# Padded tables that bring regions and weight rings to multiples of 256 bytes, and a small block of the recurrence's inverse kept in a chain buffer

## The chip, the cores and the metric

One core of one Trainium2 chip. The metric is device time in microseconds (us) of one execution; lower is better. The runs of the kernel before lie at 2445.13, 2445.94 and 2451.08 us, the median is 2445.94 us.

## What is computed

Two blocks on a sequence of 256 tokens with 2048 channels, float32 in and out. The first block has two layers: an RWKV-7 mixer (four projections, two small LoRA paths, a recurrence over time in 32 heads of 64, a projection back) and a differential attention (shared K and V, 8 heads, a gate, a projection back), each followed by a layer norm of a weighted residual. The second block puts 16 learned tokens ahead (272 rows), projects to pool, convolution and gate channels, mixes them, and ends in an MLP with a squared ReLU:

```python
y = _rwkv7_mixer(x, ...)                       # layer 0: r, k, v, g projections, recurrence, w_out
x = _layernorm(ALPHA * x + y, ...)
k_sh, v_sh = x @ w_k_shared, x @ w_v_shared
y = _diff_mixer(x, k_sh, v_sh, ...)            # layer 1
x = _layernorm(ALPHA * x + y, ...)
h = concat([meta, x]); u = rms_norm(h)
proj = u @ w_in                                # pool, conv value, conv gate, gate a, gate b
m = sigmoid(ga) * y_pool + sigmoid(gb) * y_conv
h = h + rms_norm(m @ w_o)
f = square(relu(rms_norm(h) @ w_up)) @ w_down
return (h + rms_norm(f))[META:]
```

The recurrence is computed in chunks of 64 steps. Each chunk needs the inverse of a triangular 64 x 64 matrix, put together from two 32 x 32 inverses and a product of three 32 x 32 blocks.

## The kernel before

Activations are kept transposed: channels on the 128 partitions, 16 tiles of them side by side, tokens along the row. They live in long-lived *regions* of 128 partitions (B0, B1, B2, B3, H0, L0, taken by `region`, line 196), which are used again by stage after stage under new names. The profile shows B regions as rB, H0 as rH, L0 as rL.

**Projections.** Every float32 product is made of three matmuls in a faster float format: weights and activations are split into a high part and a low rest, and `mm3` (line 313) issues high x high, high x low rest of the activation, low rest of the weight x high. The weights stream in tiles of 128 x 1024 (512 KB): the SP queue loads them into `wraw`, ScalarE copies the high part into `wh` (line 283), VectorE, in some stages every second time GpSimd, subtracts it into `wl` (line 284). Each of the three is a ring of three buffers of 4096 bytes a partition. `proj` (line 323) walks over 16 column tiles (or more) and 16 k; the weights are loaded into TensorE (128 x 128), and 256 token columns, in the second block's input projection 272, stream past them. The order of the weights is one list (line 228), from which `WS` runs ahead by its rings' depth. In V and in the MLP's down projection activations are the stationary side and 512 columns of a weight tile stream (line 127, `mm`). A matmul with one stationary and one moving tile is written acc<-moving,stationary in the profile.

In the last projection five of the last eight weight tiles are split into buffers of their own (`own0h` to `own2l` and, for the first two, parts of region L0), so that they need not wait for the ring.

**The recurrence.** `wkv(j)` (line 705) is a generator, one for each of 16 pairs of heads, run a little at every tick between the projections' matmuls. It loads what `pregen` and `invgen` stored, forms the product of two 32 x 32 blocks on TensorE, copies it to `Q` (lines 740 to 742), multiplies it by the third block and puts the result into `Z` (lines 755 to 764), and then runs a chain of four chunks (lines 807 to 842) whose left-hand matrices are in `BG`, one of three buffers of [4 chunks, 2 heads, 2, 64]. Before the change Q has a tile of its own, `wQ`, 512 bytes a partition in one buffer. `take` and `give` limit how many pairs are in a part at a time: one in the front part, which Q belongs to, and three in the chain, one for each BG buffer. BG[:, 3, 1] is the last chunk's matrix for the second head. For the last chunk the half of the chain's result that carries the state on is not read.

**Where the tiles lie.** Long-lived tiles stand one behind the other in the order of their making: `cst` (constants), `prm` and `prm1` (parameter vectors), the regions, EXH and EXL (two more slots for mixed activations), `der`, `omu`, `PC`, B2, B3, two buffers each of `mx` and `xx`, `sst` (a row of 272 sums), two small `rr`, and then the rings wraw, wh and wl. Behind them each stage opens a pool of its own. Small tiles are rounded up to 32 bytes. Start of a tile within a partition, in bytes past a multiple of 256:

| tile | before | after, as the sizes add up |
|---|---|---|
| cst | 128 | 128 |
| prm / prm1 | 224 / 32 | 0 / 0 |
| B0, B1, H0, L0, EXH, EXL | 160 | 0 |
| B2, B3, mx, xx, sst | 96 | 0 |
| wraw, wh, wl (all nine) | 224 | 0 |
| first tile of each stage's pool, among them ml | 224 | 0 |
| own0h to own2l (last stage) | 0 | 32 |
| zh, zl (pool groups) | 192 | 224 |

A row of 256 columns has 1024 bytes, so all 16 rows of a region start alike. A row of 272 has 1088, so rows of the second block's input start at 160, 224, 32, 96 and again, after the change at 0, 64, 128, 192. [...] In the projection after the attention (wbo) the high parts are in B1 and the low ones in B3; in the second block's output projection (wo) in B1 and ml; in K, Q, the gate and up in H0 and L0.

Of the kernel before, what the change touches and what calls it, by code (L numbers as in the profile page):

```python
# [10 lines left out]
F32 = mybir.dt.float32  # L11
# [8 lines left out]
SEQ = 256  # L20
NT = 16
META = 16
L2 = SEQ + META
# [9 lines left out]
P2048 = ["mu_k", "mu_v", "mu_r", "mu_g", "mu_w", "mu_a", "w0", "a0", "k_k", "k_a", "r_k", "gn_g", "gn_b",  # L33
         "ln_g0", "ln_b0", "ln_g1", "ln_b1", "g_pre", "g_post", "g_pre_mlp", "g_post_mlp"]
P1024 = ["pool_scale", "b_dw", "cln_g", "cln_b"]
CONSTS = [("ident", 128), ("istack", 64), ("bones", 128), ("sel2", 2), ("maskn", 128), ("maskg", 128),
          ("mask2", 128), ("scanm", 256), ("ones", 128), ("epow", 16)]
DIST_BIG = 1.0e30
INVQ = 500
LAG = 3  # L40
# [21 lines left out]
def shape_consts():  # L62
    p = np.arange(128)
    c = np.arange(128)
    o = {}
    o["ident"] = np.eye(128)
    o["istack"] = (p[:, None] % 64 == np.arange(64)[None, :])
    o["bones"] = (p[:, None] // 64 == c[None, :] // 64)
    o["sel2"] = (p[:, None] // 64 == np.arange(2)[None, :])
    o["maskn"] = -1.0 * (p[:, None] % 64 < c[None, :] % 64)  # L70
    o["maskg"] = (p[:, None] % 64 <= c[None, :] % 64)
    m2 = np.ones((128, 128))
    m2[:, 64:] = c[None, :64] < (p[:, None] % 64)
    o["mask2"] = m2
    o["scanm"] = np.broadcast_to((np.arange(256) % CH != 0)[None, :], (128, 256))
    o["ones"] = np.ones((128, 128))
    o["epow"] = np.full((128, 16), -0.5)
    out = np.concatenate([np.asarray(o[n], np.float32) for n, w in CONSTS], axis=1)
    q = np.arange(256)
    k = np.arange(256)  # L80
    dist = np.abs(q[:, None] - k[None, :]).astype(np.float32)
    dist = np.where(k[None, :] // CH <= q[:, None] // CH, dist, np.float32(DIST_BIG)).astype(np.float32)
    dd = np.concatenate([dist[:128, :128], dist[128:, :]], axis=1)
    return np.ascontiguousarray(out), np.ascontiguousarray(dd)
# [25 lines left out]
def body(ctx: ExitStack, tc: tile.TileContext, t: dict, out: bass.AP, dbg=None):  # L110
    nc = tc.nc
    S = ctx.enter_context(tc.tile_pool(name="S", bufs=1))
# [13 lines left out]
    def mm(o, l, r, start=True, stop=True):  # L126
        i = nc.tensor.matmul(o, l, r, start=start, stop=stop, skip_group_check=True)  # L127
        if hop["lag"]:
            hop["due"].append((hop["n"] + hop["lag"], i))

    def turn(o, i):

        nc.tensor.transpose(o, i, ident[:i.shape[0], :i.shape[0]])

    def tt(o, a, b, op, eng=None):
        return (eng or nc.vector).tensor_tensor(o, a, b, op)  # L136
# [58 lines left out]
    def region(tag, dt, shape):  # L195
        n = 1
        for v in shape[1:]:
            n *= v
        bw = BW.get(tag, NT * L2)
        assert n <= bw  # L200
        tl = S.tile([128, bw], dt, tag=tag, name=f"r{tag}")
        v = tl[:, :n]
        if len(shape) == 3:
            v = v.rearrange("p (a b) -> p a b", b=shape[2])
        elif len(shape) == 4:
            v = v.rearrange("p (a b c) -> p a b c", b=shape[2], c=shape[3])
        return v

    cst = S.tile([128, sum(w for _, w in CONSTS)], F32, tag="cst", name="cst")
    prm = S.tile([128, len(P2048), NT], F32, tag="prm", name="prm")  # L210
    prm1 = S.tile([128, len(P1024), 8], F32, tag="prm1", name="prm1")
    C = {}
    off = 0
    for n, w in CONSTS:
# [85 lines left out]
    def give(what):  # L300
        busy[what] -= 1
# [4 lines left out]
    def bank():  # L306
        yield from take("m")
        return mbank()
# [67 lines left out]
        s = n % NS  # L376
        return (H0[:, s], L0[:, s]) if s < NT else (EXH[:, s - NT], EXL[:, s - NT])

    derived = S.tile([128, 1, NT], F32, tag="der", name="der")
    omu = S.tile([128, 6, NT], F32, tag="omu", name="omu")  # L380
    PC = S.tile([64, NT, 2, 4], F32, tag="PC", name="PC")

# [21 lines left out]
    def f1(tag, cols, bufs=1, parts=128, dt=F32, name=None):  # L404
        return F1.tile([parts, cols], dt, tag=tag, name=name or tag, bufs=bufs)
# [297 lines left out]
    def wkv(j):  # L703
# [25 lines left out]
        BG, RZ, SS = BGB[j % NB], RZB[j % NB], SSB[j % NB]  # L729
# [7 lines left out]
        for c in range(4):  # L737
            mm(kp[:, c * 128:c * 128 + 128], KT[:, c], KB[:, c, 0:3:2])
        yield
        Q = f1("wQ", 128)  # L740
        nc.vector.tensor_copy(Q[32:64], qp[32:64, :128])
        nc.scalar.copy(Q[96:128], qp[96:128, :128])
        give("m")
# [11 lines left out]
        for c in range(4):  # L755
            for h in range(2):
                hs = slice(64 * h + 32, 64 * h + 64)
                mm(zp[64 * h:64 * h + 32, c * 32:c * 32 + 32], Q[hs, c * 32:c * 32 + 32], Z[hs, c, h, 32:64])
        vp = yield from bank()
# [103 lines left out]
    def wkvman():  # L863
        while wq["next"] < NT:
            j = wq["next"]
            if state["inv"] > j // 8 and wq["t"] - wq["last"] >= INTERVAL and busy.get("ld", 0) < 2:
                bg.start(wkv(j))
                wq["next"] += 1
                wq["last"] = wq["t"]
            wq["t"] += 1  # L870
            yield
# [347 lines left out]
    ul = region("L0", F32R, [128, NT, L2])  # L1219
    nc.scalar.copy(uh[:, :, 0:META], um)  # L1220
    tt(ul[:, :, 0:META], um, uh[:, :, 0:META].bitcast(F32), SUB, nc.gpsimd)
    sst = S.tile([128, L2], F32, tag="sst", name="sst")
    sq3 = {}

    def square_in(j, src, n, s2, F, eng):
# [217 lines left out]
    ss = sst[:, :SEQ]  # L1443
# [21 lines left out]
    rb = mbank()  # L1465
    for b in range(2):
        turn(rb[:, b * 128:b * 128 + 128], r[:, b:b + 1].to_broadcast([128, 128]))
    ss = S.tile([128, L2], F32, tag="sst", name="sst")[:, :SEQ]
    H = region("B3", F32, [128, NT, SEQ])
    uh = region("H0", F32R, [128, NT, SEQ])  # L1470
    ul = region("L0", F32R, [128, NT, SEQ])
# [146 lines left out]
def layout(i):  # L1618
    f = {n: np.asarray(a) for n, a in i.items()}
    o = {}  # L1620
    o["x"] = f["x"][0].T.reshape(NT, 128, SEQ).transpose(1, 0, 2)
    o["meta"] = f["meta_2"].T.reshape(NT, 128, META).transpose(1, 0, 2)
    o["consts"], o["dist"] = shape_consts()
    vec = {"mu_r": f["a_mu_proj"][0, 0], "mu_k": f["a_mu_proj"][0, 1], "mu_v": f["a_mu_proj"][0, 2], "mu_g": f["a_mu_proj"][0, 3],
           "mu_w": f["a_mu_lora"][0, 0], "mu_a": f["a_mu_lora"][0, 1], "w0": f["a_w0"][0], "a0": f["a_a0"][0],
# [31 lines left out]
def build(arrays, debug=None):  # L1657
    import concourse.bacc as _bacc

    nc = _bacc.Bacc("TRN2", target_bir_lowering=False, num_devices=1)  # L1660
    t = {}
    for name, a in arrays.items():
        t[name] = nc.dram_tensor(f"in_{name}", a.shape, mybir.dt.from_np(a.dtype), kind="ExternalInput").ap()
    out = nc.dram_tensor("out_0", (2, 128, D), F32, kind="ExternalOutput").ap()
    dbg = None
    if debug:
        dbg = {n: nc.dram_tensor(f"dbg_{n}", s, F32, kind="ExternalOutput").ap() for n, s in debug.items()}
    with tile.TileContext(nc, schedule_with_timeline_sim=True) as tc:
        body(tc, t, out, dbg)
    return nc  # L1670
# [10 lines left out]
```

## Time and profile before

| | |
|---|---|
| runs | 2445.13, 2445.94, 2451.08 us; median 2445.94 |
| profiled execution | 2448.95 us, of it 2447.1 us from the first to the last instruction |
| granted TensorE clock, mean of the span | 0.992 |
| busy: TensorE, VectorE, ScalarE, GpSimd | 2373.7, 1572.0, 1214.6, 560.9 us |
| DMA | 437.84 MB, 179 GB/s on the mean |

The profile is one execution. Engines: PE is TensorE's matmuls, PEld its weight loads, which overlap them, DVE VectorE, ACT ScalarE, POOL GpSimd, SP the queue that issues the transfers. Matmuls overlap in the pipeline: the record of one is longer than the distance to the next, so their pace is read from counts over a stretch, not from a duration.

### The profile page before, as it was taken

The page shows a single profiled execution, that of the slowest core. Times are in us where ns is not written, and L with a number is a line of the kernel's source. Part 1 is how long each engine was busy: PE and PEld are TensorE (multiplying, and loading weights), DVE is VectorE, ACT ScalarE, POOL GpSimd, SP SyncE. Part 2 cuts the span into 40 slices and gives each one's busy share as a digit, 9 for nine tenths or more (in the row PEclk, how much of TensorE's full clock was granted, in tenths as well). Part 3 has the DMA queues.
Part 4 walks back from the last instruction along what each step waited for, and adds up shares of the span by engine and source line. Part 5 has one row for each costly group of instructions (what it writes and reads, how often), then busy time and mean ns, then how long its engine had stood idle before and what let it go on. Part 6 is the DMA issues. An engine that isn't in the chain of part 4 may idle for free.

```text
span 2447.1 us, 46389 instructions
## 1 busy us (share of the span) xinstructions
PE 2373.7 (97%) x18359; PEld 2254.1 (92%) x18359; DVE 1572.0 (64%) x2675; ACT 1214.6 (50%) x2033; POOL 560.9 (23%) x583
## 2 busy tenths in 40 slices
PE   7999999999999999999999999999999999999998
PEld 6989899899978999999999999999998998998986
DVE  7788867676674455666689853454854655655655
ACT  7874556655444445554633455344544443443443
POOL 0110022331630000017766553531400000000000
PEclk9999999999999999999999999999999999999999
DMA  6577654445556654555455655555566666566655
GB/s 218 165 232 224 200 174 137 135 134 172 175 173 191 195 176 156 164 175 163 149 172 174 189 173 181 182 181 172 173 192 191 186 189 192 187 189 191 188 182 163
DMA packets 157978, 437.84 MB, mean 179 GB/s; under 512 B 45280, under 2 KB 50784, under 8 KB 157536
## 3 DMA queue, kind: packets, MB, share of 16 engines
q1 hardware_dynamic: 157760, 434.87, 57.7%
q8 instruction: 144, 2.36, 0.4%
q14 instruction: 74, 0.61, 0.1%
HBM read 418.55 MB, written 16.25 MB: 178 GB/s over the span
## 4 chain that ended last, share of the span: by engine, by line
PE 83%; DVE 5%; POOL 3%; DMA 3%; issue 2%; ACT 2%; SPq 1%; DVEq 0%; POOLq 0%; ACTq 0%
PE acc L315 58%; PE acc L127 18%; PE psm L127 5%; PE psc L127 2%; DVE wl L284 2%; POOL rB L136 1%; DMA wraw<-in_wk 1%; ACT wh L283 1%; POOL s L136 1%; DMA wraw<-in_wr 1%; POOL sst L136 1%; DVE rB L139 0%; POOL mt L136 0%; DVE rB L136 0%; DMA nd<-nb 0%
## 5 line engine op out<-in xcount | busy, mean ns | idle before, releaser
L284 DVE TENSOR_TENSOR wl<-wraw,wh 128x1024 fp32r<-128x1024 f32 x680 | 852.6, 1255 | 627.0 <-ACT wh L283 622.0
L283 ACT CAST wh<-wraw 128x1024 fp32r<-128x1024 f32 x749 | 784.2, 1048 | 880.7 <-PE acc L315 509.3
L315 PE MATMUL acc<-rH,wh 128*128 128x256 f32 (+1 forms) x4096 | 1132.9, 284 | 21.4 <-ACT wh L283 11.8
L315 PE MATMUL acc<-rL,wh 128*128 128x256 f32 (+1 forms) x3840 | 1077.3, 283 | 9.9 <-DVE rL L136 5.9
L315 PE MATMUL acc<-rH,wl 128*128 128x256 f32 (+1 forms) x3840 | 1078.3, 284 | 6.4 <-POOL wl L284 4.7
L315 PEld LDWEIGHTS acc<-rH,wh 128*128 128x128 f32 x4096 | 765.6, 190 | 27.4 <-ACT wh L283 12.7
L315 PEld LDWEIGHTS acc<-rL,wh 128*128 128x128 f32 x3840 | 726.0, 189 | 14.8 <-DVE rL L136 8.0
L315 PEld LDWEIGHTS acc<-rH,wl 128*128 128x128 f32 x3840 | 728.3, 190 | 9.9 <-POOL wl L284 5.7
L127 PE MATMUL acc<-wh,rB 128*128 128x512 f32 x984 | 306.0, 391 | 0.0
L315 PE MATMUL acc<-rB,wh 128*128 128x256 f32 x1024 | 233.5, 281 | 1.4 <-DVE mt L139 1.4
L136 POOL TENSOR_TENSOR r<-r,cst 128x4 f32<-128x4 f32 (+1 forms) x34 | 37.5, 1104 | 844.0 <-DVE r L145 688.1
L127 PEld LDWEIGHTS acc<-wh,rB 128*128 128x128 f32 x984 | 184.8, 188 | 40.8
L315 PE MATMUL acc<-rB,wl 128*128 128x256 f32 x768 | 214.0, 281 | 7.5 <-DVE wl L284 7.5
L284 POOL TENSOR_TENSOR wl<-wraw,wh 128x1024 fp32r<-128x1024 f32 x69 | 170.6, 2472 | 143.2 <-ACT wh L283 134.5
L127 PE MATMUL acc<-wl,rB 128*128 128x512 f32 x492 | 194.6, 396 | 0.0
L315 PEld LDWEIGHTS acc<-rB,wh 128*128 128x128 f32 x1024 | 174.1, 188 | 2.2 <-DVE mt L139 1.7
L315 PEld LDWEIGHTS acc<-rB,wl 128*128 128x128 f32 x768 | 144.1, 188 | 9.4 <-DVE wl L284 9.3
L127 PEld LDWEIGHTS acc<-wl,rB 128*128 128x128 f32 x492 | 92.5, 188 | 19.0
L139 DVE SCALAR_TENSOR_TENSOR psm<-aconv,wdw,psm 128x256 f32<-128x256 f32 x240 | 102.3, 483 | 0.8
L136 POOL TENSOR_TENSOR asq<-asq 128x256 f32<-128x256 f32 x8 | 5.9, 736 | 330.9 <-ACT asq L148 330.9
L315 PE MATMUL acc<-ml,wh 128*128 128x256 f32 x256 | 72.1, 282 | 0.0
L136 POOL TENSOR_TENSOR sst<-sst,sqt 128x256 f32<-128x256 f32 (+1 forms) x44 | 44.0, 1000 | 87.5 <-ACT sqt L148 86.3
(335 smaller groups left out, 2549.5 us busy)
## 6 DMA issues: line engine op xcount, KB each, us to landing
wraw<-in_wup SPq DMA_DIRECT2D x128, 512.0 KB, 4.3
wraw<-in_wdn SPq DMA_DIRECT2D x128, 512.0 KB, 3.6
wraw<-in_win SPq DMA_DIRECT2D x112, 512.0 KB, 3.6
wraw<-in_wqg SPq DMA_DIRECT2D x64, 512.0 KB, 3.6
wraw<-in_wk SPq DMA_DIRECT2D x32, 512.0 KB, 4.3
wraw<-in_wv SPq DMA_DIRECT2D x32, 512.0 KB, 4.7
wraw<-in_wr SPq DMA_DIRECT2D x32, 512.0 KB, 3.7
wraw<-in_wg SPq DMA_DIRECT2D x32, 512.0 KB, 3.6
```

Source lines behind the costliest of these rows:

```text
L127: i = nc.tensor.matmul(o, l, r, start=start, stop=stop, skip_group_check=True)
L136: return (eng or nc.vector).tensor_tensor(o, a, b, op)
L139: return nc.vector.scalar_tensor_tensor(o, a, s, b, op0, op1)
L283: c = nc.scalar.copy(h, r)
L284: s = e.tensor_tensor(l, r, h.bitcast(F32), SUB)
L315: i = nc.tensor.matmul(ps, w, x, start=f, stop=e, skip_group_check=True)
```

## The change

Three of the long-lived tables get longer, so that what lies behind them moves: 14 columns of zeros at the end of the constants, three more rows in `prm`, four in `prm1`, a second row in `derived`, and `sst` is taken as 304 columns of which 272 are used. The views that the code works on are the same. The two copies that made `wQ` write into BG[:, 3, 1] of the pair's own chain buffer, and the tile wQ is gone. The chain's mask (the product with maskg) and the copy of the transposed blocks write that buffer later.

```diff
--- before.py
+++ after.py
@@ -34,7 +34,7 @@
          "ln_g0", "ln_b0", "ln_g1", "ln_b1", "g_pre", "g_post", "g_pre_mlp", "g_post_mlp"]
 P1024 = ["pool_scale", "b_dw", "cln_g", "cln_b"]
 CONSTS = [("ident", 128), ("istack", 64), ("bones", 128), ("sel2", 2), ("maskn", 128), ("maskg", 128),
-          ("mask2", 128), ("scanm", 256), ("ones", 128), ("epow", 16)]
+          ("mask2", 128), ("scanm", 256), ("ones", 128), ("epow", 16), ("fill", 14)]
 DIST_BIG = 1.0e30
 INVQ = 500
 LAG = 3
@@ -75,6 +75,7 @@
     o["scanm"] = np.broadcast_to((np.arange(256) % CH != 0)[None, :], (128, 256))
     o["ones"] = np.ones((128, 128))
     o["epow"] = np.full((128, 16), -0.5)
+    o["fill"] = np.zeros((128, 14))
     out = np.concatenate([np.asarray(o[n], np.float32) for n, w in CONSTS], axis=1)
     q = np.arange(256)
     k = np.arange(256)
@@ -207,8 +208,8 @@
         return v
 
     cst = S.tile([128, sum(w for _, w in CONSTS)], F32, tag="cst", name="cst")
-    prm = S.tile([128, len(P2048), NT], F32, tag="prm", name="prm")
-    prm1 = S.tile([128, len(P1024), 8], F32, tag="prm1", name="prm1")
+    prm = S.tile([128, len(P2048) + 3, NT], F32, tag="prm", name="prm")[:, :len(P2048)]
+    prm1 = S.tile([128, 2 * len(P1024), 8], F32, tag="prm1", name="prm1")[:, :len(P1024)]
     C = {}
     off = 0
     for n, w in CONSTS:
@@ -376,7 +377,7 @@
         s = n % NS
         return (H0[:, s], L0[:, s]) if s < NT else (EXH[:, s - NT], EXL[:, s - NT])
 
-    derived = S.tile([128, 1, NT], F32, tag="der", name="der")
+    derived = S.tile([128, 2, NT], F32, tag="der", name="der")
     omu = S.tile([128, 6, NT], F32, tag="omu", name="omu")
     PC = S.tile([64, NT, 2, 4], F32, tag="PC", name="PC")
 
@@ -737,7 +738,7 @@
         for c in range(4):
             mm(kp[:, c * 128:c * 128 + 128], KT[:, c], KB[:, c, 0:3:2])
         yield
-        Q = f1("wQ", 128)
+        Q = BG[:, 3, 1].rearrange("p a t -> p (a t)")
         nc.vector.tensor_copy(Q[32:64], qp[32:64, :128])
         nc.scalar.copy(Q[96:128], qp[96:128, :128])
         give("m")
@@ -1219,7 +1220,7 @@
     ul = region("L0", F32R, [128, NT, L2])
     nc.scalar.copy(uh[:, :, 0:META], um)
     tt(ul[:, :, 0:META], um, uh[:, :, 0:META].bitcast(F32), SUB, nc.gpsimd)
-    sst = S.tile([128, L2], F32, tag="sst", name="sst")
+    sst = S.tile([128, 304], F32, tag="sst", name="sst")[:, :L2]
     sq3 = {}
 
     def square_in(j, src, n, s2, F, eng):
@@ -1465,7 +1466,7 @@
     rb = mbank()
     for b in range(2):
         turn(rb[:, b * 128:b * 128 + 128], r[:, b:b + 1].to_broadcast([128, 128]))
-    ss = S.tile([128, L2], F32, tag="sst", name="sst")[:, :SEQ]
+    ss = S.tile([128, 304], F32, tag="sst", name="sst")[:, :SEQ]
     H = region("B3", F32, [128, NT, SEQ])
     uh = region("H0", F32R, [128, NT, SEQ])
     ul = region("L0", F32R, [128, NT, SEQ])
```

## Rows read from the trace of the kernel before

**Rows 1.** The page's head and its part 1: busy time of each engine, share of the span and number of instructions.

```profile
span 2447.1 us, 46389 instructions
...
PE 2373.7 (97%) x18359; PEld 2254.1 (92%) x18359; DVE 1572.0 (64%) x2675; ACT 1214.6 (50%) x2033; POOL 560.9 (23%) x583
```

**Rows 2.** The page's part 4: the chain that ended last, shares of the span by engine and by line.

```profile
PE 83%; DVE 5%; POOL 3%; DMA 3%; issue 2%; ACT 2%; SPq 1%; DVEq 0%; POOLq 0%; ACTq 0%
PE acc L315 58%; PE acc L127 18%; PE psm L127 5%; PE psc L127 2%; DVE wl L284 2%; POOL rB L136 1%; DMA wraw<-in_wk 1%; ACT wh L283 1%; POOL s L136 1%; DMA wraw<-in_wr 1%; POOL sst L136 1%; DVE rB L139 0%; POOL mt L136 0%; DVE rB L136 0%; DMA nd<-nb 0%
```

**Rows 3.** Steady stretches, instructions of line 315 alone (the three matmuls of each k). Columns: the stretch in us from the span's start; its length; TensorE busy us (number of matmuls); weight loads busy us (number); granted clock; DMA share; GB/s. In order of time: the attention-free mixer's output projection wao (622), K (800), the input projection with 272 columns (1260), the gates (1340), the pool output projection (1545), the output projection with ml (1625), up in quarters one to four (1765, 1910, 2085, 2260); 1085 is the projection after the attention, wbo.

```profile
622.00:638.00 16.00, 16.00 (x139) 16.00 (x138) 1.00 0.59 183
800.00:860.00 60.00, 60.00 (x532) 60.00 (x531) 1.00 0.62 193
1545.00:1570.00 25.00, 25.00 (x223) 25.00 (x222) 1.00 0.65 203
1765.00:1800.00 35.00, 35.00 (x311) 35.00 (x311) 1.00 0.69 210
1910.00:1980.00 70.00, 70.00 (x597) 70.00 (x596) 1.00 0.60 187
2085.00:2150.00 65.00, 65.00 (x555) 65.00 (x554) 1.00 0.60 187
2260.00:2320.00 60.00, 60.00 (x512) 60.00 (x511) 1.00 0.64 186
1085.00:1140.00 55.00, 54.92 (x462) 54.71 (x461) 1.00 0.60 183
1625.00:1690.00 65.00, 65.00 (x553) 65.00 (x552) 1.00 0.63 191
1340.00:1390.00 50.00, 50.00 (x425) 50.00 (x424) 1.00 0.63 190
1260.00:1310.00 50.00, 50.00 (x399) 50.00 (x398) 1.00 0.60 180
```

**Rows 4.** The same columns for line 127 (matmuls of 512 columns) in the first and second down quarter.

```profile
1850.00:1890.00 40.00, 40.00 (x177) 32.81 (x176) 1.00 0.63 191
2000.00:2050.00 50.00, 50.00 (x221) 41.00 (x219) 1.00 0.60 192
```

**Rows 5.** Line 315 in the K projection, 800 to 860 us: count, shortest/median/longest duration in ns, first and last start in us, shapes.

```profile
L315 PEld LDWEIGHTS acc<-rH,wl x177: 187/188/188, 799.9 to 859.7; 128*128 128x128 f32 x177
L315 PE MATMUL acc<-rH,wl x177: 276/276/276, 800.0 to 859.8; 128*128 128x256 f32 x177
...
L315 PEld LDWEIGHTS acc<-rL,wh x177: 187/188/188, 800.1 to 859.9; 128*128 128x128 f32 x177
```

**Rows 6.** The same for the second up quarter, 1910 to 1980 us.

```profile
L315 PE MATMUL acc<-rH,wl x199: 281/281/281, 1909.8 to 1979.7; 128*128 128x256 f32 x199
...
L315 PEld LDWEIGHTS acc<-rL,wh x199: 187/188/188, 1909.9 to 1979.9; 128*128 128x128 f32 x199
...
L315 PEld LDWEIGHTS acc<-rH,wl x199: 192/192/192, 1910.0 to 1980.0; 128*128 128x128 f32 x199
```

**Rows 7.** Groups of TensorE's instructions in the last projection, 2405 to 2436 us. Columns: line, engine, operation, out<-in, shapes, count | busy us (overlaps counted once), mean ns of one | idle time before.

```profile
L127 PE MATMUL acc<-wh,rB 128*128 128x512 f32 x51 | 16.4, 392 | 0.0
...
L127 PE MATMUL acc<-rL,rB 128*128 128x512 f32 x24 | 6.6, 392 | 0.0
L127 PE MATMUL acc<-own1h,rB 128*128 128x512 f32 x8 | 2.8, 397 | 0.0
L127 PE MATMUL acc<-own2h,rB 128*128 128x512 f32 x8 | 2.8, 396 | 0.0
L127 PE MATMUL acc<-own0h,rB 128*128 128x512 f32 x8 | 2.8, 395 | 0.0
```

**Rows 8.** The same columns, 2340 to 2447 us: the split of a weight tile on VectorE (line 284) and the copy on ScalarE (line 283), into ring buffers and into own buffers.

```profile
L284 DVE TENSOR_TENSOR wl<-wraw,wh 128x1024 fp32r<-128x1024 f32 x28 | 34.3, 1225 | 29.7 <-ACT wh L283 29.6
...
L284 DVE TENSOR_TENSOR own0l<-wraw,own0h 128x1024 fp32r<-128x1024 f32 x1 | 1.2, 1226 | 2.0 <-ACT own0h L283 2.0
...
L283 ACT CAST wh<-wraw 128x1024 fp32r<-128x1024 f32 x27 | 28.3, 1050 | 37.4 <-PE acc L127 28.1 <-PE acc L315 5.0 <-DMA wraw<-in_wdn 3.0
...
L283 ACT CAST own0h<-wraw 128x1024 fp32r<-128x1024 f32 x1 | 1.1, 1050 | 2.2 <-DMA wraw<-in_wdn 2.2
```

**Rows 9.** The first 40 us. Columns: the stretch; its length; busy us (number of instructions) of TensorE, of weight loads, VectorE, ScalarE, GpSimd; granted clock; DMA share; GB/s.

```profile
0.00:20.00 20.00, 12.11 (x71) 10.75 (x72) 12.61 (x28) 13.64 (x26) 1.81 (x11) 1.00 0.90 304
20.00:40.00 20.00, 15.23 (x96) 12.10 (x95) 15.28 (x40) 12.94 (x28) 0.00 (x0) 1.00 0.82 233
```

**Rows 10.** DMA issues: out<-in, issuing queue, count, KB each, median us from issue to landing.

```profile
wraw<-in_wk SPq DMA_DIRECT2D x32, 512.0 KB, 4.3
...
cst<-in_consts SPq DMA_DIRECT2D x1, 553.0 KB, 11.2
```

**Rows 11.** Instructions that write or read the tile wQ, then the masks that write wBG: count, shortest/median/longest ns, first and last start in us.

```profile
L127 PE MATMUL psm<-zb,wQ x256: 191/191/212, 278.4 to 551.0; 32*32 32x32 f32 x128
L741 DVE COPY wQ<-psm x16: 282/283/284, 270.6 to 544.5; 32x128 f32<-32x128 f32 x16
L742 ACT COPY wQ<-psm x16: 257/258/259, 272.1 to 545.1; 32x128 f32<-32x128 f32 x16
...
L136 DVE TENSOR_TENSOR wBG<-psm,cst x32: 647/691/693, 273.4 to 558.9; 128x512 f32<-128x512 f32 x32
```

## The prediction

> **What bounds the kernel now.** I read the page first, then the chain of waits, then the stretches in which TensorE runs without a gap. TensorE is busy for 97% of the span, far above the other engines [rows 1], and the chain that ended last lies on it for 83%, 58% on line 315 alone [rows 2]. So a nanosecond per matmul counts almost in full, and a transfer or a copy counts only where TensorE stands still.
>
> A busy TensorE is not yet a fast one, so the next view is the pace. I take it as (stretch + one record of 0.28 us) / count, because a matmul that straddles an edge is counted too. With 256 moving columns the pace is 60.28/532 = 113.3 ns in the K projection, 113.4 ns in the first quarter of the up projection (35.28/311), but 117.7 ns in the second quarter (70.28/597) and the same in the third and fourth [rows 3]. [...] The other paces are 119.7 ns in the projection after the attention, 118.1 where ml streams, 118.3 in the gates, and 126.0 ns for 272 columns [rows 3]. With 512 columns it is 229 ns, which is 114.5 per 256 [rows 4].
>
> The quarters of the up projection issue the same instructions on the same tiles, yet run at two paces. In the fast one every weight load takes 188 ns; in the slow one exactly one of the three (that of rH with wl) takes 192 ns and each matmul 281 instead of 276 [rows 5, 6]. This looks like two streams of TensorE, the moving rows and the weights loaded for the next matmul, that get in each other's way or not, in a rhythm that holds until something disturbs it. Where the tiles start is what can shift such a rhythm, and in the last projection it seems to: matmuls of 512 columns whose moving rows start 0 bytes past a multiple of 256, with weights at 160, show records of 395 to 397 ns (own0h, own1h, own2h), those with both at 160 (rL) 392, and those with 224 against 160 (wh) also 392 [rows 7].
>
> **The change part by part.** *The starts.* Before, moving rows of the regions start at 160 or 96 past a multiple of 256 and the weights at 224; after, both at 0 in every stage whose rows are 1024 bytes apart. Rows 272 wide step by 64 modulo 256 and keep all four distances from the weights, so I expect nothing from the input projection and the gates, 2688 matmuls [rows 3]. For the rest the trace has no row of 0 against 0. [...] The nearest row in kind is rL, equal starts of both, at 392 [rows 7], which is the best there. I therefore take the better of the two paces that the kernel already shows, 113.3 ns, for all stages with equal starts:
>
> - three quarters of up at 117.7: each 16 columns x 16 x 3 = 768 matmuls, so 3 x 768 x 4.4 ns = 10.1 us;
> - the projection after the attention: 768 x 6.4 ns = 4.9 us;
> - the projection with ml: 768 x 4.8 ns = 3.7 us;
> - the 512-column stages: V and the four down quarters, 5 x 384 = 1920 x (229 - 226.7) = 4.4 us;
> - the seven 256-column projections of the two mixers that are broken up by small matmuls (k, v, r, g and out of the first, q and g of the second; 5376 matmuls). I take them halfway between the two paces now, 2.2 ns: 11.8 us;
> - K, the pool and conv outputs and the first up quarter are at 113.4 already: 0 to 1 us.
>
> That is 35 us. In the first 690 us TensorE also waits for weights, mixes and the recurrence (small, but the waits then absorb part of it), so I take 4 us off: **31 us**.
>
> *Vector and scalar work.* The same split of a weight tile takes 1226 ns into own0l (start 0) and 1225 into wl (start 224), and the copies take 1050 both [rows 8]. Where a tile starts costs these engines nothing that shows; 0, whichever way.
>
> *Transfers.* The first 40 us are where transfers set the pace (DMA engines 90% and 82% busy, TensorE 12.1 of 20 us [rows 9]). DMA lies on 3% of the chain, 73 us [rows 2]. A row of 4096 bytes that starts at 224 touches 17 blocks of 256 bytes, at 0 it touches 16; if the time went with that, 1/17 of 73 = 4 us would be gained, and if not, 0. The tiles x and lw1 that lead the first stretch start elsewhere within their rows, so I take 0 and keep 4 for the range. The table of constants grows by 56 bytes a partition, 7 KB on 553 KB that land in 11.2 us [rows 10]: 0.14 us behind other transfers, nothing. The parameter tables load the same bytes into a longer tile.
>
> *The small block.* Q's two copies (283 ns on VectorE, 258 ns on ScalarE, 16 each [rows 11]) now write into BG's last block. No instruction is added; what changes is whom they wait for. Before, the matmuls that read the previous head pair's Q; now, the chain's last matmuls on that BG buffer, three head pairs back. TensorE runs in order and the chain must have given its place before the pair starts, so these matmuls stand ahead of the ones that produce Q, which the copies wait for anyway. Queued behind the VectorE copy are KA's mask and the weight splits; none waits longer. The later mask that overwrites the block (one of the 691 ns ones [rows 11]) must follow the 256 small matmuls that read Q; it already waits for a product that TensorE issues after them. Cost 0; if that cover failed, 16 pairs x (283 + 258) ns = 8.7 us would be the most.
>
> The sum is made against the profiled execution: 2448.95 - 31 = 2418; that run is 3 us above the median of 2445.94, so on the median's scale 2415 us.
>
> [...]
>
> **The rivals.**
>
> *Nothing moves (24%).* The two paces come from the rhythm alone and the starts do not enter. For it: one set of tiles shows both paces [rows 5, 6]. Against: the odd distances (119.7, own) stand out [rows 3, 7]. Time: 2446, down to 2438 if only the two odd projections (4.9 + 3.7) come right, so 2438 to 2450.
>
> *Slower (29%).* Equal starts put the two streams in step, so that the slow rhythm becomes the only one: every equal-start stage runs at 117.7 or the 119.7 of the odd projection. It decides as soon as a moving row and a weight row begin at the same place at the same moment; before, they were 64 bytes apart in most stages. At 117.7: K, the outputs and the first up quarter lose 4.4 ns on 3 x 768 matmuls (10 us), the mixers 2.2 on 5376 (12), less 2 from the odd projection: 2446 + 20 = 2466. At 119.7 another 2 ns on about 10,000: 2486; with 512 columns slower as own's are (4 ns on 1920) 2494.
>
> [...]
>
> **How the numbers follow.** My forecast, the fast rhythm everywhere, gets 35%: 2415 us, its own range 2398 to 2432. About 0.3%, 7 us, is what a measurement of this kernel can tell from no change (the three runs lie 6 us apart). Faster by more: 35% + 12% + 6% of the "nothing" case = 53%. Within: 16% of that case and 2% of the slow one = 18%. Slower: 27% + 2% = 29%. The range runs from 2398 (2446 less all 35 us, less 4 of the transfers and some 9 for scatter and paces a little under 113.3) to 2486 (the slow case at 119.7); left out are the deep case and own's end of the slow one, some 16%.
>
> **What would show it.** Right: the second to fourth up quarters at 113.3 ns with all weight loads at 188, the projection after the attention near 113, the gates still near 118, wl and wh splits unchanged, Q's copies with no new waiter. Wrong: the up quarters still at 117.7 (nothing), the K projection at 117.7 or above (slower), any 256-column stretch below 112 (deeper), or new idle time of VectorE ahead of Q.

## The result: slower by 1.2%, and the profile after

The kernel after takes 2477.99 us (median of 4 runs, 2474.52 to 2479.54), the kernel before beside it 2445.53 us (4 runs, 2443.47 to 2451.08): ratio 1.0118, 95% interval 1.0103 to 1.0133. The profiled execution of after took 2474.52 us. Lines of the code stand one further down than before: L316, L128, L285 and L284 were L315, L127, L284 and L283.

The page's head and its part 1, which answer to [rows 1]:

```profile
span 2472.7 us, 46380 instructions
...
PE 2409.6 (97%) x18359; PEld 2296.2 (93%) x18359; DVE 1572.7 (64%) x2675; ACT 1214.5 (49%) x2033; POOL 562.1 (23%) x583
```

The span of the profiled executions grew by 25.6 us, less than the 32.5 us between the medians: the profiled run of before lies 3.4 us above its median, that of after 3.5 us below its own. The number of matmuls is the same, VectorE, ScalarE and GpSimd are as busy as before, but TensorE is busy for 36 us more and its weight loads for 42 us more: the same instructions take longer on that engine alone. The chain that ended last has the shares that it had, to one point in a hundred [rows 2]:

```profile
PE 82%; DVE 6%; POOL 4%; issue 3%; DMA 2%; ACT 2%; SPq 1%; DVEq 0%; POOLq 0%; ACTq 0%
```

Now the steady stretches, line 316 alone, columns as in [rows 3]. In order: the first mixer's output projection (622), K (800), wbo (1090), 272 columns (1260), the gates (1340), the pool output projection (1560), wo with ml (1660), up in quarters one to four (1790, 1940, 2110, 2290).

```profile
622.00:638.00 16.00, 16.00 (x136) 16.00 (x135) 1.00 0.58 188
800.00:860.00 60.00, 60.00 (x502) 60.00 (x502) 1.00 0.59 184
1090.00:1130.00 40.00, 40.00 (x336) 40.00 (x335) 1.00 0.59 184
1260.00:1310.00 50.00, 49.75 (x395) 49.53 (x394) 1.00 0.56 175
1340.00:1390.00 50.00, 50.00 (x424) 50.00 (x423) 1.00 0.60 190
1560.00:1590.00 30.00, 30.00 (x253) 30.00 (x252) 1.00 0.59 188
1660.00:1710.00 50.00, 50.00 (x419) 50.00 (x419) 1.00 0.58 180
1790.00:1830.00 40.00, 40.00 (x335) 40.00 (x335) 1.00 0.66 189
1940.00:2000.00 60.00, 60.00 (x502) 60.00 (x501) 1.00 0.59 184
2110.00:2170.00 60.00, 60.00 (x503) 60.00 (x502) 1.00 0.57 182
2290.00:2350.00 60.00, 60.00 (x502) 60.00 (x501) 1.00 0.59 184
```

By the rule of the prediction, (stretch + one record of 0.28 us)/count, K runs at 60.28/502 = 120.1 ns, where it was 113.3, and the up quarters at 120.1 too, where three ran at 117.7. From the start of a stretch's first matmul to that of its last, which has no such edge, it is 120.0 ns in each 256-column stage with rows of 1024 bytes; the paces below without a working are taken so. The gates stay at 118.3. The granted clock is 1.00 in all these stretches, as before, and 0.992 on the mean of the span, as before. Only the 512 columns gained: in the first and second down quarter, (40 + 0.39)/178 = 226.9 and 50.39/223 = 226.0 ns, 226.7 from start to start, against 228.9 before [rows 4].

```profile
1870.00:1910.00 40.00, 40.00 (x178) 33.14 (x177) 1.00 0.62 192
2030.00:2080.00 50.00, 50.00 (x223) 41.39 (x222) 1.00 0.62 196
```

The durations in K, 800 to 860 us, which answer to [rows 5]: all loads take 192 ns, where all took 188, and the matmuls 283 instead of 276. In the slow rhythm of before one load in three was so long [rows 6]; now each is. The up quarters show the same numbers (192 and 283).

```profile
L316 PE MATMUL acc<-rH,wh x168: 283/283/284, 799.8 to 859.9; 128*128 128x256 f32 x168
L316 PEld LDWEIGHTS acc<-rL,wh x168: 191/192/193, 799.8 to 859.9; 128*128 128x128 f32 x168
...
L316 PEld LDWEIGHTS acc<-rH,wl x167: 191/192/193, 799.9 to 859.7; 128*128 128x128 f32 x167
```

**Where the 25.6 us lie**, by the start of a stage's first long unbroken run of matmuls, in us from the span's start:

| from | before | after | added in the part before it |
|---|---|---|---|
| K | 780.7 | 782.2 | 1.5 (mixers' k, v, r, g, out; V) |
| Q and gate projections, third column | 883.3 | 890.6 | 5.8 (K and two columns of these) |
| wbo | 1073.8 | 1087.1 | 6.0 |
| pool and conv outputs | 1533.8 | 1549.4 | 2.3 (wbo, 272 columns, gates) |
| wo | 1617.3 | 1635.1 | 2.2 |
| second up quarter | 1900.0 | 1922.7 | 4.9 (wo, first up, first down) |
| end | 2447.1 | 2472.7 | 2.9 (up 1.8 + 1.8 + 1.7, down and tail -2.4) |

In the first 690 us TensorE became 10.4 us busier (651.5 to 661.9 us), but at the start of K only 1.5 us are lost: in that part it also stands idle for others, and the idle time became shorter by most of the rest.

### The profile page after: what moved, and what is told of

It reads as the page before. It is cut to its first block, busy times and chain, and to the rows that moved or that the text cites. A ratio compares the mean times of both kernels' runs of the same rounds, so it can differ in the third digit from the quotient of the medians.

```text
span 2472.7 us, 46380 instructions
## 1 busy us (share of the span) xinstructions
PE 2409.6 (97%) x18359; PEld 2296.2 (93%) x18359; DVE 1572.7 (64%) x2675; ACT 1214.5 (49%) x2033; POOL 562.1 (23%) x583
## 4 chain that ended last, share of the span: by engine, by line
PE 82%; DVE 6%; POOL 4%; issue 3%; DMA 2%; ACT 2%; SPq 1%; DVEq 0%; POOLq 0%; ACTq 0%
PE acc L316 57%; PE acc L128 17%; PE psm L128 4%; PE psc L128 2%; DVE wl L285 2%; POOL rB L137 1%; DMA wraw<-in_wk 1%; POOL s L137 1%; ACT wh L284 1%; POOL mt L137 1%; DMA wraw<-in_wv 1%; DVE rB L140 1%; POOL sst L137 0%; DVE rB L137 0%; PE psm L316 0%
## 5 line engine op out<-in xcount | busy, mean ns | idle before, releaser
L285 DVE TENSOR_TENSOR wl<-wraw,wh 128x1024 fp32r<-128x1024 f32 x680 | 851.6, 1253 | 643.6 <-ACT wh L284 639.1
L284 ACT CAST wh<-wraw 128x1024 fp32r<-128x1024 f32 x749 | 783.8, 1048 | 903.5 <-PE acc L316 499.1
L316 PE MATMUL acc<-rH,wh 128*128 128x256 f32 (+1 forms) x4096 | 1147.9, 287 | 16.6 <-ACT wh L284 10.7
L316 PE MATMUL acc<-rH,wl 128*128 128x256 f32 (+1 forms) x3840 | 1092.1, 287 | 4.9 <-POOL wl L285 3.5
L316 PE MATMUL acc<-rL,wh 128*128 128x256 f32 (+1 forms) x3840 | 1089.7, 286 | 7.1 <-DVE rL L137 3.6
L316 PEld LDWEIGHTS acc<-rH,wh 128*128 128x128 f32 x4096 | 777.6, 192 | 21.9 <-ACT wh L284 11.7
L316 PEld LDWEIGHTS acc<-rL,wh 128*128 128x128 f32 x3840 | 736.6, 192 | 10.8 <-DVE rL L140 5.3
L316 PEld LDWEIGHTS acc<-rH,wl 128*128 128x128 f32 x3840 | 735.4, 192 | 8.1 <-POOL wl L285 4.3
L128 PE MATMUL acc<-wh,rB 128*128 128x512 f32 x984 | 304.7, 390 | 0.0
L316 PE MATMUL acc<-rB,wh 128*128 128x256 f32 x1024 | 236.1, 284 | 1.2 <-DVE mt L140 1.2
L316 PE MATMUL acc<-rB,wl 128*128 128x256 f32 x768 | 216.7, 285 | 6.3 <-DVE wl L285 6.2
L128 PEld LDWEIGHTS acc<-wh,rB 128*128 128x128 f32 x984 | 184.8, 188 | 38.2
L285 POOL TENSOR_TENSOR wl<-wraw,wh 128x1024 fp32r<-128x1024 f32 x69 | 170.9, 2477 | 146.3 <-ACT wh L284 140.0
L128 PE MATMUL acc<-wl,rB 128*128 128x512 f32 x492 | 193.2, 393 | 0.0
L316 PEld LDWEIGHTS acc<-rB,wh 128*128 128x128 f32 x1024 | 177.5, 192 | 1.6 <-DVE mt L140 1.4
L316 PEld LDWEIGHTS acc<-rB,wl 128*128 128x128 f32 x768 | 146.7, 192 | 7.9 <-DVE wl L285 7.7
L128 PEld LDWEIGHTS acc<-wl,rB 128*128 128x128 f32 x492 | 92.4, 188 | 19.2
L316 PE MATMUL acc<-ml,wh 128*128 128x256 f32 x256 | 72.4, 283 | 0.0
```

The costliest lines, as they stand in the source:

```text
L284: c = nc.scalar.copy(h, r)
L285: s = e.tensor_tensor(l, r, h.bitcast(F32), SUB)
L316: i = nc.tensor.matmul(ps, w, x, start=f, stop=e, skip_group_check=True)
```

## The experiments

The theories: **D**, the pace hangs on the distance of the moving row's start from the weights' start, modulo 256 bytes; **E**, on the starts being even (a multiple of 256) in themselves; **Q**, the small block costs time in the recurrence; **R**, within one distance there are two rhythms, and a disturbance chooses. D64 is D with a period of 64 bytes. A distance is the moving start less the weights' start. The kicks below add matmuls whose result nobody reads; each shows in the profile as two weight loads and two matmuls, as the 128 that the kernel issues on wQ show as 256 [rows 11].

**q_only**: the kernel before, with the small block moved and no table changed.

```diff
-        Q = f1("wQ", 128)
+        Q = BG[:, 3, 1].rearrange("p a t -> p (a t)")
```

> The kernel before with the small block in the chain buffer alone; every tile starts where it did. Theory D (the distance between the start of the moving rows and that of the weights, modulo 256, sets TensorE's pace): nothing, 2443 to 2450 us, second up quarter at 117.8 ns, K at 113.3. Theory E (starts at multiples of 256 are themselves slow): the same, 2443 to 2450. Theory Q (the small block or the order of the work costs it): most of the 32 us, 2470 to 2480.

Measured: 2449.45 us (2442.78 to 2453.58), ratio 1.0001 [0.9988, 1.0014], and K at 60.28/532 = 113.3 ns as before. Q falls: the loss is the tables'.

**eq160**: Q as above, `derived` with 2 rows and `sst` with 32 columns more, so that regions, B2, B3 and rings all start at 160: equal, but not even.

> Regions at 160 past a multiple of 256 (B2 and B3 moved there too), rings at 160: as equal as in the changed kernel, but no start is a multiple of 256. Theory D: all up quarters and K at 120.0 ns, weight loads of 192 ns, 512 columns at 226.7 ns, 2472 to 2482 us. Theory E: as before or better, 113.3 to 117.8 ns, 2430 to 2450 us. Theory Q: 2470 to 2480 but with the old paces and idle time of TensorE in the recurrence.

Measured: 2475.92 us, ratio 1.0105 [1.0087, 1.0123], not to be told from after. K and the second up quarter, line 315, columns as in [rows 3]:

```profile
800.00:860.00 60.00, 60.00 (x503) 60.00 (x502) 1.00 0.59 184
1940.00:2000.00 60.00, 60.00 (x502) 60.00 (x502) 1.00 0.57 183
```

120.0 ns, 512 columns at 226.7, and all weight loads at 192: all that the change did, at starts of 160. E falls; what counts is that both start alike. One of the three loads in the second up quarter (the other two show the same):

```profile
L315 PEld LDWEIGHTS acc<-rH,wh x168: 192/192/192, 1939.8 to 2000.0; 128*128 128x128 f32 x168
```

**m0_w64** and **m0_w192**: regions at 0 as in after, the rings moved away by 64 or by 192 bytes. The distance of the regions' rows is then 192, as in most stages before, or 64.

```diff
# m0_w64                                        # m0_w192: prm1 + 11 rows, sst + 16 columns
+    prm1 = S.tile([128, len(P1024) + 3, 8], ...)[:, :len(P1024)]
+    derived = S.tile([128, 2, NT], ...)
+        Q = BG[:, 3, 1].rearrange("p a t -> p (a t)")
+    sst = S.tile([128, L2 + 48], ...)[:, :L2]
```

> Regions at 0, rings at 64: the moving rows start 192 past the weights modulo 256, the distance of the kernel before, with every region at a multiple of 256. Theory D: the two old paces 113.3 and 117.8 ns, 512 columns at 228.9 ns, 2440 to 2455 us. Theory E: 120 ns because the regions are at multiples of 256, 2470 to 2480 us. Theory Q: 2470 to 2480.

> Regions at 0, rings at 192: the moving rows start 64 past the weights for 256 columns and, in the 512-column stages, the other way round by 192. Theory D: a pace of its own that is not 120.0 ns everywhere (113.3 to 118.0 ns, as the 512-column stages of the kernel before had this distance and lost only a little), 2425 to 2460 us. Theory E: 120 ns, 2470 to 2480 us.

Measured: m0_w64 2447.63 us, ratio 0.999 [0.9979, 1.0002]; m0_w192 2466.76 us, ratio 1.0065 [1.0044, 1.0085]. The regions lie as in after, and at distance 192 the whole loss is gone: K is at 113.3 ns and the second up quarter at 117.8, as in before. Line 315 of m0_w64:

```profile
800.00:860.00 60.00, 60.00 (x532) 60.00 (x531) 1.00 0.67 194
1910.00:1980.00 70.00, 70.00 (x597) 70.00 (x596) 1.00 0.60 188
```

At 64 it is not gone, and the time lies 7 us above the range that D had given: m0_w192 shows 60.28/512 = 117.7 ns in K and up, and in the second down quarter, where the weight tile moves and the distance is 192, 80.39/344 = 233.7 (233.3 from start to start). But the fast pace occurs at 64 as well, in a few short stretches; in the mixer's output projection, the last of the three lines of line 315, (11 + 0.28)/100 = 112.8, from start to start 113.3 ns. Line 315, then line 127:

```profile
800.00:860.00 60.00, 60.00 (x512) 60.00 (x511) 1.00 0.60 189
1940.00:2000.00 60.00, 60.00 (x512) 60.00 (x511) 1.00 0.61 185
601.00:612.00 11.00, 11.00 (x100) 11.00 (x99) 1.00 0.77 250
```

```profile
2010.00:2090.00 80.00, 80.00 (x344) 64.12 (x343) 1.00 0.62 186
```

Since 0 differs from 64 and 192, D64 falls too. The slow pace at 64 has no long loads, though: in m0_w192's second up quarter all three take 187 or 188 ns, the matmuls 279 or 280, so a load of 192 ns is not the sign of every slow pace.

```profile
L315 PEld LDWEIGHTS acc<-rH,wl x171: 187/187/187, 1939.9 to 1999.9; 128*128 128x128 f32 x171
```

**m0_w128, m0_w32, m0_w160, m0_w224, m0_w96**: the other distances in steps of 32, by the same tables (`prm1` + 11 rows and `sst` + 0, 40, 8, 24 columns; for m0_w96 + 3 rows and 56), with two or three runs each.

> Regions at 0, rings at 128: moving and weight rows start 128 apart both ways round. Theory D (distance modulo 256): its own pace, the same in all stages with rows of 1024 bytes; in the kernel before, the projection that mixed this distance with the old one ran at 120 ns, so 118 to 120 ns, 2460 to 2485 us; gates at 118.3 as ever. Theory D64 (distance modulo 64 alone, multiples of 64 all alike): 120 ns as with equal starts.

> Regions at 0, rings at 32: moving rows start 224 past the weights for 256 columns, 32 past them for 512. Theory D: a pace of its own; the pool groups of the kernel before had this distance and ran at about 118.4 ns, so 117 to 119 ns, 2455 to 2475 us, and the gates, whose four distances are now odd multiples of 32, leave 118.3. Theory D64: 113.3 to 117 ns, since the blocks of 64 bytes no longer coincide, 2420 to 2445 us.

> Regions at 0, rings at 160: moving rows start 96 past the weights for 256 columns, 160 past them for 512. Theory D: a pace between 113.3 and 120 ns of its own, 2430 to 2480 us, with the 512 columns at 226.7 to 235 ns. Theory D64: the same paces as with rings at 32.

> Regions at 0, rings at 224: moving rows start 32 past the weights for 256 columns, 224 past them for 512. Theory D: a pace of its own, 113.3 to 120 ns, 2430 to 2480 us. Theory D64: the same paces as with rings at 32 and 160.

> Regions at 0, rings at 96: moving rows start 160 past the weights for 256 columns, 96 past them for 512; the last of the eight distances in steps of 32 bytes. Theory D (each distance modulo 256 has its own pace or paces): one or two steady paces between 113.3 and 120.0 ns, most likely 117 to 120 as its neighbours 128 and 192 have mostly, 512 columns near 233 to 234 ns as the own buffers had, 2455 to 2490 us. Theory D64 (modulo 64 alone): like rings at 32, 118.3 ns.

Measured: m0_w128 2477.65 us (ratio 1.0127 [1.0098, 1.0156]), m0_w32 2472.63 (1.0107 [1.0077, 1.0136]), m0_w160 2489.95 (1.0177 [1.0148, 1.0207]), m0_w224 2463.13 (1.007 [1.0048, 1.0093]), m0_w96 2470.76 (1.0091 [1.0071, 1.0112]). All times but that of m0_w160, 10 us above, lie within the ranges that D had given. The paces from start to start, in ns, with the kernels above put in; "and" means that one profiled execution, or two kernels of the same distance, show both:

| distance | 256 columns | 512 columns |
|---|---|---|
| 0 | 120.0 | 226.7 |
| 32 | 116.7 and 117.8 | 233.3 |
| 64 | 113.3 (short stretches) and 117.8 | 228.9 and 233.3 |
| 96 | 120.0 | 233.3 |
| 128 | 118.7 and 120.0 | 232.4 and 233.3 |
| 160 | 117.3 and 118.7 | 234.3 |
| 192 | 113.3 and 117.8 | 233.3 |
| 224 | 118.3 | 233.3 |

Line 315 of m0_w224 (distance 32), K and the second up quarter, 60.28/516 = 116.8; and of m0_w128, the second and third up quarter, 60.28/502 = 120.1 and then 118.7, the same work on the same tiles:

```profile
800.00:860.00 60.00, 60.00 (x516) 60.00 (x515) 1.00 0.61 186
...
1940.00:2000.00 60.00, 60.00 (x517) 60.00 (x516) 1.00 0.63 187
```

```profile
1940.00:2000.00 60.00, 60.00 (x502) 60.00 (x501) 1.00 0.60 182
2110.00:2170.00 60.00, 60.00 (x508) 60.00 (x507) 1.00 0.61 186
```

So D holds, with no simple order over the distances, and a multiple of 256 between two streams is among the worst for 256 columns and the best for 512. That the distance alone counts, and not the two places, is shown for 0 (after and eq160) and for 192 (before and m0_w64, where the rings lie 256 bytes farther from the regions); each other distance was run at one pair of places. The gates, whose rows of 1088 bytes go through four distances, stay at 118.3, or 118.9 where the four are odd multiples of 32.

**kick**: the kernel before, with twelve small matmuls of 2, 32, 64 or 128 columns strewn in the second to fourth up quarter.

```diff
+        if up["q"] and j % 4 == 1:
+            kick = mbank()
+            w = (2, 32, 64, 128)[(j // 4 + up["q"]) % 4]
+            mm(kick[:, 0:w], FH[:, j - 1, 0:128].bitcast(F32), C["ones"][:, 0:w])
```

> The kernel before with one additional small matmul (2, 32, 64 or 128 columns, into a free bank, its result unused) after columns 1, 5, 9 and 13 of the second to fourth up quarter, 12 in all, 0.2 us each. Theory R (at the old distance two rhythms are possible, and what disturbs TensorE picks one): after some of the 12 the pace turns from 117.8 to 113.3 ns and holds until the next; 2436 to 2448 us. Rival (something of the later quarters themselves, transfers or the other engines, holds them at 117.8): 117.8 after all 12, 2446 to 2453 us.

Measured: 2448.0 us, ratio 0.9997 [0.9985, 1.0008]; nothing gained in sum, and the time fits both ranges, but the pace goes up and down. Line 315 in the second up quarter, ahead of the first kick and behind each (of 32, 64, 128 and 2 columns):

```profile
1904.00:1914.00 10.00, 10.00 (x90) 10.00 (x90) 1.00 0.61 199
1915.00:1937.00 22.00, 22.00 (x189) 22.00 (x189) 1.00 0.63 192
1938.00:1959.00 21.00, 21.00 (x188) 21.00 (x186) 1.00 0.66 195
1960.00:1981.00 21.00, 21.00 (x181) 21.00 (x180) 1.00 0.61 185
1983.00:1993.00 10.00, 10.00 (x91) 10.00 (x90) 1.00 0.65 202
```

In order, 114.2 (113.6 from start to start; the edge weighs most in so short a stretch), 117.9, 113.2, 117.6 and 113.0 ns: two rhythms at one distance, and each holds until the next disturbance. R's first half is shown. In all three quarters the stretch was fast behind 2 and 64 columns and slow behind 32 and 128, so I took the size for what chooses; the next run shows otherwise.

**kick2**: the kernel before, with one matmul of 2 columns behind the first column of each of these quarters.

```diff
+        if up["q"] and j == 1:
+            kick(FH[:, 0, 0:128].bitcast(F32))      # 2 columns against C["ones"]
```

> The kernel before with one extra matmul of 2 columns after the first column of each of the second to fourth up quarters, its result unused; nothing moves. Theory 'two rhythms' (at a distance of 192 bytes a small matmul picks the pace, and the pace then stays): the three quarters run at 113.3 ns per 256 columns to their end instead of 117.8, about 3 x 720 x 4.4 ns = 9.5 us less, under 1 us for the extra matmuls: 2436 to 2442, ratio 0.995 to 0.998. Rival 'phase' (what the small matmul picks depends on the phase it meets): some quarters stay at 117.8: 2441 to 2450, ratio 0.998 to 1.002.

Measured: 2451.21 us (2448.1 to 2455.11), ratio 1.0016 [1.0004, 1.0028], 1 us above the range of "phase". "Phase" held: all three quarters stayed slow. Line 318 here is the three matmuls' line; the second quarter ahead of the kick and behind it, and the same in the third:

```profile
1898.00:1908.00 10.00, 10.00 (x91) 10.00 (x90) 1.00 0.65 194
1910.00:1985.00 75.00, 75.00 (x639) 75.00 (x638) 1.00 0.60 188
2078.00:2088.00 10.00, 10.00 (x90) 10.00 (x90) 1.00 0.70 206
2090.00:2165.00 75.00, 75.00 (x639) 75.00 (x638) 1.00 0.61 186
```

The quarters began fast by themselves (113.6 from start to start, over 96 matmuls), where those of before were slow from their first matmul on, and the kick of 2 columns put them at 75.28/639 = 117.8, in all three. In the run before the same kick had done the opposite three times. The kick's size does not choose; what does, stays open. (That a kick swaps the two paces would fit 17 of the 18 in the up quarters of kick, kick2 and best; the one of 64 columns behind the fast start of the third quarter left it fast. In best's wbo the first kick left the slow pace slow.) In kick2 the first three down quarters ran at 233.3 instead of 228.9 as well, 3 x 384 x 4.4 = 5 us, and the first up quarter at 117.8; it and the first down quarter lie ahead of the first kick.

**best**: all moving rows of 1024 bytes in the projections put 192 bytes past the rings (Q as above, `derived` 2 rows, `sst` + 48, ml 48 columns in), and the 2-column kick in wbo, wo and the up quarters. In the down stages the roles change, so their distance is 64, as before.

> All 1024-byte-pitch moving rows put 192 bytes past their weight rings (down rows too), Q in the chain's block, and extra matmuls of 2 columns in two mixer projections and in the second to fourth up quarters. Theory 'distance and two rhythms': 256 columns at 113.3 ns in these stages too, about -9.5 us in the up quarters, -5 and -3.5 us in the mixers' projections, less what the 512-column stages lose at 233.3 against 228.9 (1920 x 4.4 ns = 8 us if they lie at a distance that runs so): 2425 to 2440, ratio 0.992 to 0.998. Rival 'phase': 2440 to 2450, ratio 0.998 to 1.002.

Measured: 2450.42 us (2447.95 to 2458.76), ratio 1.0014 [0.9998, 1.0031]. The rival again: the up quarters began fast and fell to 75.28/640 = 117.6 behind the kick. So did wo: with all its rows at distance 192 its first 283 matmuls ran at 113.4 to 113.6, and only behind the kick at 117.8. Wbo was mostly at 117.8, and K this time at 60.28/511 = 118.0 (117.8 from start to start). The same tables without the kicks were not run. No version beats the kernel before by more than the scatter. Line 318, K, wo ahead of its kick and behind it, and the second up quarter:

```profile
800.00:860.00 60.00, 60.00 (x511) 60.00 (x511) 1.00 0.62 188
...
1624.00:1644.00 20.00, 20.00 (x179) 20.00 (x178) 1.00 0.72 219
1660.00:1710.00 50.00, 50.00 (x427) 50.00 (x426) 1.00 0.61 188
...
1918.00:1993.00 75.00, 75.00 (x640) 75.00 (x639) 1.00 0.59 187
```

## Why the prediction was wrong

The forecast was 2415 us; the time, 2478, lies between the two that the rival "Slower" gave, 2466 and 2486. Point by point:

**The step that failed** is the choice of a pace for equal starts: "the nearest row in kind is rL, equal starts of both, at 392 [rows 7]... I therefore take the better of the two paces that the kernel already shows, 113.3 ns". That row has 512 columns, and the text gives no reason why 256 should go the same way. For 512 it told the truth: equal starts gave 226.7 ns, the best of all distances, and 1920 x 2.2 = 4.2 us were gained, near the 4.4 forecast. For 256 columns the same starts gave 120.0, close to the slowest 256-column pace of the text (119.7), and not 113.3. The last projection of after, columns as in [rows 7], shows the 512-column rule once more: wh and rL, equal to their weights, at 390 and 391, and the own tiles, 32 bytes past theirs, at 394 to 397.

```profile
L128 PE MATMUL acc<-wh,rB 128*128 128x512 f32 x51 | 16.3, 390 | 0.0
...
L128 PE MATMUL acc<-rL,rB 128*128 128x512 f32 x24 | 6.6, 391 | 0.0
...
L128 PE MATMUL acc<-own0h,rB 128*128 128x512 f32 x8 | 2.9, 397 | 0.0
L128 PE MATMUL acc<-own2h,rB 128*128 128x512 f32 x8 | 2.8, 396 | 0.0
L128 PE MATMUL acc<-own1h,rB 128*128 128x512 f32 x8 | 2.8, 394 | 0.0
```

**The terms, forecast and measured.** Three up quarters: -10.1, became +5.3 (768 x 2.2 = 1.7 each). wbo: -4.9; its steady run went from 118.8 to 120.0 ns from start to start, 768 x 1.2 = +0.9. The 119.7 by the count took up its broken places. wo: -3.7, became +1.5 from its first unbroken run on (90.0 us to its last matmul, then 91.5). The broken-up projections: -11.8; the part from Q's third column to wbo added 6.0 instead, and the first 780 us only 1.5. Their halfway pace had no row, and the trace of before speaks against it: seven of the nine unbroken runs of over 60 matmuls between 883 and 1061 us are at 113.5 from start to start, two at 117.8, so little was to be gained there and much to be lost. K, outputs, first up quarter: 0 to -1; they lost most, 6.7 ns a matmul, 768 x 6.7 = 5.1 us each by count, for they had been in the fast rhythm; the table above has 5.8 for K with two columns behind it, 2.2 for the outputs, and the first up quarter lost 3.9 (98.1 us from its first matmul to the first of down, then 102.0).

**What held.** That starts matter: eq160 against q_only differ by 26 us by starts alone, with loads of 192 ns for 188. That the moving rows and the weights get in each other's way fits the distance as the cause, but no trace shows a read, and it stays an inference. The gates and the 272 columns, forecast unchanged, are unchanged. The splits and copies too: 1224 and 1052 ns here, against 1225 and 1050 [rows 8], 2340 to 2447 us there and 2366 to 2472 here.

```profile
L285 DVE TENSOR_TENSOR wl<-wraw,wh 128x1024 fp32r<-128x1024 f32 x28 | 34.3, 1224 | 29.5 <-ACT wh L284 29.5
L284 ACT CAST wh<-wraw 128x1024 fp32r<-128x1024 f32 x27 | 28.4, 1052 | 37.0 <-PE acc L128 26.4 <-PE acc L316 3.7 <-issue 2.9
```

The transfers of wk land in 4.3 us as before [rows 10]: an even start bought nothing that shows. Q's copies take what they took [rows 11], and q_only shows the move to cost nothing (ratio 1.0001). From the fourth pair on the products that make Q start 8 us or more after the last matmul on the BG buffer of three pairs back, in before as in after (the fourth pair's at 338.9 against 327.2 us, and at 334.2 against 322.3), the order that the prediction counts on.

```profile
wraw<-in_wk SPq DMA_DIRECT2D x32, 512.0 KB, 4.3
```

```profile
L742 DVE COPY wBG<-psm x16: 283/284/285, 269.6 to 543.4; 32x128 f32<-32x128 f32 x16
L743 ACT COPY wBG<-psm x16: 257/258/261, 270.6 to 544.0; 32x128 f32<-32x128 f32 x16
```

**The rivals.** "Slower" named what came: every equal-start stage of 256 columns on one slow pace. It was right in place and near in price, and it had 29% because I let a row of another shape outweigh it. That the streams fall in step, its reason, is not shown, and two things in its price were luck or wrong: 119.7, so near the 120.0 that came, is a count with wbo's pauses in it, 118.8 from start to start; and the 512 columns that it would have had slower became faster. The trace of before had nearer rows, which I read for their oddness and not for their distance: the two 256-column stages in which a third of the matmuls leave the distance 192, wbo (B3 at 96 against 224: 128) and wo (ml at 224 against 224: 0, equal starts), were among the slow ones, 119.7 and 118.1 by the count [rows 3], and neither was at 113.3. The text says that the trace has no row of 0 against 0; it had one of 224 against 224, in ml. Eq160 shows that equal starts away from 0 run as those at 0 do. "Nothing moves" falls with eq160. The 12% in the chances, and the "deep case" that the range leaves out, are for a pace below 113.3 ns, which no run shows: no 256-column stage of any kernel was below 113.3 ns from start to start.

**What stays open.** Why 113.3 at 192 and 120.0 at 0, inside TensorE, no trace shows. Nor is it known what sets the rhythm, or whether it changes between executions of one kernel: each kernel was profiled once. At distance 192, K ran at 113.3 in before, q_only, m0_w64 and kick2 and at 117.8 in kick and best, though kick and kick2 differ from before only in work long after K.

## What to carry to other kernels

In a kernel like this one, where TensorE is the bound (its matmuls busy for 97% of the span, its weight loads for 92% [rows 1]), the distance between the starts of the moving rows and of the weights modulo 256 bytes is a parameter of the kernel, worth 6% of the pace here (113.3 ns at 192, 120.0 at 0); lay a table out only with a measurement of each distance for the shape at hand, and don't expect a rounder number to be the better one. A row of the trace prices a change only for its own shape: the same starts were best for 512 columns (226.7 ns) and among the worst for 256 (120.0). And where stages of the same work run at two paces, as the first up quarter of before at 113.4 ns and the other three at 117.8, count on the slower one.

## What the runs showed that I had not expected

- Padding a few tables by some hundred bytes, far away from the matmuls, moved the time by anything from nothing that can be told (m0_w64, ratio 0.999) to +1.8% (m0_w160).
- Each distance has a pace of its own that repeats to 0.3 ns between steady stages and kernels, and at 32, 64, 128, 160 and 192 bytes two of them, 1.1 to 4.4 ns apart. Each holds over hundreds of matmuls, but for the fast one at 64, seen over some hundred at a time.
- One matmul of 2 columns can send the pace either way, and it stays there: from 113.6 to 117.8 in kick2, from 117.8 to 113.5 in kick.
- The kernels at distance 192 scatter more: 2442.78 to 2453.58 us in 10 runs of q_only, against 2473.77 to 2478.76 in 4 of eq160. Two rhythms would do that, but with such numbers of runs it is only a hint.
